# Moving the attention output's gatings between the weight splits, and turning the gate logits by full tiles

## The chip, the core and the metric

The kernel runs on one core of one Trainium2 chip. The metric is the device time of one execution in microseconds, shown as the median of the runs. A core has a matrix engine (PE), a vector engine (DVE), an activation engine (ACT), a general engine (POOL) and a queue engine (SP). Each takes its own instructions in order; semaphores tie them together. SP, ACT and POOL also issue DMA transfers, all of which run on the same 16 DMA engines.

## The reference, cut to what matters

The program is a trunk of two layers over 256 tokens of width 1024. Each layer normalises its input, projects it with one wide weight, runs two token mixers beside each other (a gated delta rule in both directions over chunks, here called branch a, and differential softmax attention, branch b), gates each, merges both and projects back.

```
proj = h @ w_in[l]
(q_a, k_a, v_a, ab_a, z_a, q_b, k_b, v_b, z_b, gate_a, gate_b) = jnp.split(proj, SPLIT_IDX, axis=-1)
y_a = gated_delta_branch(q_a, k_a, v_a, ab_a, z_a, ...)
y_b = diff_attention_branch(q_b, k_b, v_b, z_b, ...)     # rmsnorm(o) * (1 - lambda_init) * silu(z_b)
merged = (jax.nn.sigmoid(gate_a) * (y_a @ w_pa[l]) + jax.nn.sigmoid(gate_b) * (y_b @ w_pb[l]))
x = x + merged @ w_out[l]
```

Two pieces are touched by the change: `ab_a`, 32 columns that hold the logits of beta and of the decay g for 8 heads and two directions, and the last line of branch b, the gating of the attention output by silu(z_b) ahead of `w_pb`.

## The kernel before, in words

All matrix work is kept near float32: each weight of 256 rows by 512 columns (a "part", four to a projection, numbered kp 0 to 3) is loaded by SP as `raw`, rounded by ACT to `hi` (L308), and DVE takes the rest `lo = raw - hi` (L310). The activations `hT` are split the same way, and the PE adds hi·hi, hi·lo and lo·hi (L324 to L326). So every part costs one load, one ACT cast, one DVE subtraction and 12 matmuls of 128 by 512 (two 128-row blocks, two token tiles m, three products). `raw` has three buffers, `hi` and `lo` two each, so a part's load starts when the `lo` three parts earlier is done.

The order of instructions on each engine is set by the framework's list scheduler, which places instructions by its own estimate of time. The kernel steers it with `behind(x)`, which lets an instruction be placed only after instruction x on the same engine, and with `mark[name, kp]`, which keeps the pair (cast, subtraction) of a part.

The stage around the change is the projection of the two merge gates, `gb` and then `ga`. Between their matmuls the PE does the rest of branch a: `y64p`, `zt`, `y128p` and `zt` join the blocks of a triangular inverse U (`join`, L928 to L978), then for each group of four heads and each direction `y1p`, `sp`, `ks`, `y2p`, `qs` and `po` run the chunk recurrence (`chunks`, L992 to L1033). ACT copies each result out of PSUM: `A<-y1p` (L1000) is the left operand of `sp`, and `ktm<-sp` (L1006) that of `ks`. DVE turns 32 by 32 blocks of U into `T64` (L954), which `y128p` reads.

In the same stage DVE gates the attention output. It is held as `ob[i]`, with i the half of heads (0 or 1) and m the token tile, so four pieces (i, m). For each piece `gate_yb` does four products of 128 by 128 (L1197), a DVE turn into `zb` (L249, in `send`), one store of 256 KB to DRAM (`bny_yb<-zb`, L251) and four loads of 64 KB back (`zb<-bny_yb`, L257, in `fetch`). Store and loads are issued on POOL, and the loads wait for the store to land. `split_B` then makes `ybT`: ACT the upper part (L263), DVE the lower (L265), placed behind the casts and subtractions of `ga0` kp 2 and 3 and of `ga1` kp 2 and 3. `ybT` is first read by the projection `pb`, after all of `ga`. The POOL queue also carries the bounce of the query norms (`qdr<-qss` L1049, `qss<-qdr` L1052), which `key_sums` fills by squares `tb_q`.

The gate logits are made early in each layer: 16 matmuls give `abp`, 64 rows (two addends of 32 columns each) by 256 tokens; ACT copies it to `abT`; two matmuls of the 64-row `abT` with `id2`, two stacked 32 by 32 identities, turn it and add the two addends (L636); one DVE copy takes it to `ab` (L638).

Of the kernel before, what the change touches and what calls it, by code (L numbers as in the profile page):

```python
# [8 lines left out]
F32 = mybir.dt.float32  # L9
# [3 lines left out]
ALU = mybir.AluOpType  # L13
# [4 lines left out]
P = 128  # L18
DM = 1024
KT = DM // P  # L20
SEQ = 256
NM = SEQ // P
# [23 lines left out]
C_QB, C_KB, C_VB, C_ZB, C_GA, C_GB = 4128, 5152, 6176, 7200, 8224, 9248  # L46
# [3 lines left out]
def hybrid_encoder(  # L50
# [19 lines left out]
    V, S, G, T = nc.vector, nc.scalar, nc.gpsimd, nc.tensor  # L70

    def pool(name, bufs=1, space=None):
        kw = {} if space is None else {"space": space}
        return ctx.enter_context(tc.tile_pool(name=name, bufs=bufs, **kw))

    const = pool("const")
    wpool = pool("wpool")
    big = pool("big")
    work = pool("work", 2)
# [15 lines left out]
    def bank_c(name):  # L95
        return ps_c.tile([P, 512], F32, tag="c", name=name)
# [4 lines left out]
    def last(ap, n):  # L101
        return ap.unsqueeze(ap.ndim).to_broadcast(list(ap.shape) + [n])

    mark = {}


    ident = const.tile([P, P], F32, name="ident")
# [1 line left out]
    G.memset(ident, 1.0)  # L109
    G.affine_select(out=ident, in_=ident, compare_op=ALU.is_equal, fill=0.0,  # L110
                    base=0, pattern=[[1, P]], channel_multiplier=-1)
    id2 = const.tile([64, 32], F32, name="id2")
    V.tensor_tensor(id2, ident[0:64, 0:32], ident[0:64, 32:64], ALU.add)
    G.memset(tri, 1.0)
    for d, sg in ((0, 1), (1, -1)):
        G.affine_select(out=tri[:, d, :], in_=tri[:, d, :], compare_op=ALU.is_ge,
# [28 lines left out]
    def e4(name, tag):  # L145

        return [big.tile([P, NM, 512], F32, tag=tag, name=f"{name}_{i}", bufs=2) for i in range(2)]

    def heads4(ap):
        return ap.rearrange("p (h e) -> p h e", e=P)  # L150
# [103 lines left out]
    def fetch(tb, dd, after):  # L254
        for j in range(4):
            with behind(after):
                G.dma_start(out=tb[blk(j)], in_=dd[:, :, j].rearrange("i t x -> t i x"))  # L257
# [9 lines left out]
    def pair(nm):  # L267
        return [big.tile([P, 2, 4, SEQ], F32R, tag="p8", name=f"{nm}_{i}", bufs=4) for i in range(2)]

    def behind(ins):  # L270
        return nullcontext() if ins is None else tc.issue_after(ins)
# [43 lines left out]
    def proj_tm(act, w, c0, n, evac, nm, places=(None,) * 4, spare=(), later=None, turned=(), between=None,  # L315
                banks=None, held=None, first=(), raws={}):

        accs = (banks or banks2)(f"pp_{nm}")
        for kt, hi, lo in weights(w, c0, n, nm, places, later=later, spare=spare, turned=turned, held=held,
                                  first=first, raws=raws):  # L320
            for m in range(NM):
                ts_ = slice(m * P, (m + 1) * P)
                o = accs[m][:, :n]
                T.matmul(o, act[kt // 4][:, 0, kt % 4, ts_], hi, start=kt == 0, stop=False)  # L324
                T.matmul(o, act[kt // 4][:, 0, kt % 4, ts_], lo, start=False, stop=False)  # L325
                mark["proj"] = T.matmul(o, act[kt // 4][:, 1, kt % 4, ts_], hi, start=False,  # L326
                                        stop=kt == KT - 1).ins
                mark["done", nm, kt] = mark["proj"]
        if between:
            between()  # L330
        for m in range(NM):
            evac(m, accs[m][:, :n])
# [174 lines left out]
    for l in range(DEPTH):  # L507
# [109 lines left out]
        ab = small.tile([P, NM, 32], F32, tag="ab", name=f"ab{l}")  # L617
# [9 lines left out]
        abp = ps_p.tile([P, 512], F32, tag="p", name=f"abp{l}")  # L627
        for kt in range(KT):
            for part in range(2):
                T.matmul(abp[0:64, :SEQ], wabr[:, kt, :], hT[kt // 4][:, part, kt % 4, :],  # L630
                         start=kt == 0 and part == 0, stop=kt == KT - 1 and part == 1)
        abT = work.tile([64, SEQ], F32, tag="w2c", name=f"abT{l}", bufs=3)
        mark["ab"] = S.copy(abT, abp[0:64, :SEQ]).ins
        abq = bank_c(f"abq{l}")
        for m in range(NM):
            T.matmul(abq[:, m * 32 : (m + 1) * 32], abT[:, m * P : (m + 1) * P], id2,  # L636
                     start=True, stop=True)
        V.tensor_copy(ab.rearrange("p m c -> p (m c)"), abq[:, :64])  # L638

        a_ = small.tile([P, NM, 32], F32, tag="ga_", name=f"ga_{l}")  # L640
        V.tensor_scalar(a_[:, :, 0:16], ab[:, :, 0:16], -1.0, None, ALU.mult)
# [524 lines left out]
        for p in range(4):  # L1166
            z_part((zb, za)[p // 2], (C_ZB, C_ZA)[p // 2], ("zb", "za")[p // 2], p % 2)
            for h in (2 * p, 2 * p + 1):
                at = place((3, 7, 11, 15, 19, 23, 27, 31)[h])
# [21 lines left out]
        def gated(o_, z_, r_, nw_, yT, nm, tiles=range(NM), after={}, halves_=range(2), sent=None):  # L1191
            for i in halves_:
                for m in tiles:
                    zv, ov = heads4(z_[i][:, m, :]), o_(i, m)
                    for j in range(4):
                        with behind(after.get((i, m))):
                            V.scalar_tensor_tensor(ov[:, j, :], ov[:, j, :],  # L1197
                                                   r_[:, m, 4 * i + j : 4 * i + j + 1],
                                                   zv[:, j, :], ALU.mult, ALU.mult)
                    if sent is None:  # L1200
                        split_T(yT[i], ov, m, f"{nm}{i}", w=nw_)
                    else:
                        tb = z_[i][:, m, :].rearrange("p (j x) -> p j x", j=4)
                        sent[i, m] = tb, send(tb, ov, f"{nm}{i}{m}")

        def gate(c_base, nm, tag, between=(None, None), places=((None,) * 4,) * 2, first=(),
                 raws=({}, {})):
            gt = []
            for i in range(2):
                def evac_g(m, ps, i=i):  # L1210
                    if not gt:
                        gt.extend(e4(nm, tag))
                    S.activation(gt[i][:, m, :], ps, AF.Tanh, scale=0.5)
                proj_tm(hT, wl, c_base + 512 * i, 512, evac_g, f"{nm}{i}", places[i], between=between[i],
                        later={1: (0, None)} if i and places[i][1] is not None else None,
                        first=first, raws=raws[i])
            return gt
# [27 lines left out]
        V.scalar_tensor_tensor(rb, rb, 0.5 * (1.0 - lam0), r0, ALU.mult, ALU.mult)  # L1245

        ybT, yb_sent = pair(f"ybT{l}"), {}
        def gate_yb(i):
            at = [mark[f"ga{l}0", 1 + m][1] if i else mark[f"gb{l}1", 2 + m][1] for m in range(NM)]
            gated(lambda i, m: heads4(ob[i][:, m, :]), zb, rb, nw[:, 1:2], ybT, f"yb{l}",  # L1250
                  after={(i, m): at[m] for m in range(NM)}, halves_=(i,), sent=yb_sent)
            for m in range(NM):
                fetch(*yb_sent[i, m], None)

        gate_yb(0)
        gta = gate(C_GA, f"ga{l}", "eo", (lambda: gate_yb(1), None))
        for i, m in ((0, 0), (0, 1), (1, 0), (1, 1)):
            split_B(ybT[i], yb_sent[i, m][0], m, nw[:, 1:2], mark[f"ga{l}{i}", 2 + m])
        branch(ybT, w_pb[l], gtb, f"pb{l}")
# [73 lines left out]
        for s_, _ in enumerate(o_last):  # L1333
            if more:
                prenorm(s_, xt, wb, l + 1)
            else:

                m = min(s_, 1)
# [6 lines left out]
                else:  # L1345
                    cs = slice(256 * (s_ - 1), 256 * s_)
                    part = ss[:, 1:2] if s_ == 1 else small.tile([P, 1], F32, tag="xsl", name="xsl", bufs=1)
# [49 lines left out]
```

## Time and profile before

| | |
|---|---|
| median of 3 runs | 743.0 us (742.79 to 744.36) |
| the profiled execution | 742.73 us, span 740.8 us |
| granted clock of the matrix engine | 0.997 |
| PE busy | 732.1 us, 99% of the span, 5034 records |
| DVE, ACT, POOL busy | 588.5, 479.5, 140.9 us |
| gate stage, layer 0 (first `pp_ga` to last) | about 254 to 296 us |
| gate stage, layer 1 | about 616 to 658 us |

Matrix records overlap in the trace: a 128 by 512 product is shown with 0.39 us, but the next starts 0.23 us later. So what a step of the PE costs is read from the distance between starts. A float32 product is shown as two records ("x4" are two products), a turn by the PE as one.

### The profile page before, as it was taken

The numbers are of one execution on the slowest core, as the hardware profiler recorded it, in microseconds if no ns is written. First come the engines' busy times: TensorE is split into PE (matmuls) and PEld (weight loads), VectorE is DVE, ScalarE is ACT, GpSimd is POOL, SyncE is SP. The second block draws the span as 40 slices with busy tenths as digits, with TensorE's granted clock in tenths as the row PEclk, the third lists the DMA queues.
The fourth block names the chain that finished last, engine by engine and source line by source line (L and its number), as shares of the span: only waits on it lengthen the run. The fifth ranks groups of instructions, "written<-read, shape, count | busy, mean of one in ns | idle before, by whom it ended". The sixth has DMA issues, their size and how long they took to land.

```text
span 740.8 us, 13649 instructions
## 1 busy us (share of the span) xinstructions
PE 732.1 (99%) x5034; PEld 635.6 (86%) x5034; DVE 588.5 (79%) x1119; ACT 479.5 (65%) x1018; POOL 140.9 (19%) x223
## 2 busy tenths in 40 slices
PE   9999999999999999999999999999999999999996
PEld 6999889987888899888889899889788888998885
DVE  8696898999986885578667769999999769728782
ACT  6666875667876586645456578555787748665552
POOL 6004110112022433100000150202110514311000
PEclk9999999999999999999999999999999999999998
DMA  8755667776766473567674466767766736436641
GB/s 264 239 173 171 172 181 195 209 207 203 208 181 163 136 208 104 173 205 246 201 234 138 129 192 184 212 175 236 200 173 197 203 116 196 150 124 204 213 142 57
DMA packets 73732, 135.43 MB, mean 183 GB/s; under 512 B 12912, under 2 KB 13921, under 8 KB 73666
## 3 DMA queue, kind: packets, MB, share of 16 engines
q1 hardware_dynamic: 64750, 113.65, 51.6%
q0 software_dynamic: 7936, 19.35, 9.1%
q10 hardware_dynamic: 980, 1.58, 0.6%
q8 instruction: 39, 0.64, 0.4%
q14 instruction: 27, 0.22, 0.1%
HBM read 125.53 MB, written 9.01 MB: 182 GB/s over the span
## 4 chain that ended last, share of the span: by engine, by line
PE 96%; ACT 2%; issue 1%; DVE 1%; POOLq 0%; POOL 0%; DVEq 0%; ACTq 0%
PE pp_vb L369 4%; PE pp_qk L325 4%; PE pp_qk L326 3%; PE pp_qk L324 3%; PE sc L1067 2%; PE pp_o L369 2%; PE pp_za L325 2%; PE pf_k L385 2%; PE pf_v L385 2%; PE pf_v L389 2%; PE pp_ga L324 2%; PE pp_gb L324 2%; PE pp_zb L324 2%; PE pf_q L387 2%; PE pf_k L389 2%; PE pf_k L387 2%
## 5 line engine op out<-in xcount | busy, mean ns | idle before, releaser
L325 PE MATMUL pp_qk<-lo_qk,hT 128*128 128x512 f32 x128 | 50.5, 394 | 0.3
L326 PE MATMUL pp_qk<-hi_qk,hT 128*128 128x512 f32 x128 | 49.9, 390 | 0.0
L310 DVE TENSOR_TENSOR lo_qk<-raw_qk,hi_qk 128x1024 fp32r<-128x1024 f32 x32 | 39.1, 1221 | 12.0 <-ACT hi_qk L308 11.7
L324 PE MATMUL pp_qk<-hi_qk,hT 128*128 128x512 f32 x128 | 45.1, 393 | 0.0
L308 ACT CAST hi_qk<-raw_qk 128x1024 fp32r<-128x1024 f32 x28 | 29.4, 1049 | 23.4 <-PE pp_qk L326 12.7
L1077 ACT ACTIVATE es<-sc,mx 128x256 f32<-128x256 f32 x64 | 29.6, 473 | 19.5 <-DVE mx L1075 19.5
L385 PE MATMUL pf_q<-hT,hi_q 128*128 128x256 f32 x128 | 36.1, 285 | 0.0
L387 PE MATMUL pf_q<-hT,hi_q 128*128 128x256 f32 x128 | 35.9, 284 | 0.0
L385 PE MATMUL pf_k<-hT,hi_k 128*128 128x256 f32 x128 | 35.9, 286 | 0.0
L387 PE MATMUL pf_k<-hT,hi_k 128*128 128x256 f32 x128 | 35.9, 285 | 0.0
L385 PE MATMUL pf_v<-hT,hi_v 128*128 128x256 f32 x128 | 35.8, 285 | 0.0
L387 PE MATMUL pf_v<-hT,hi_v 128*128 128x256 f32 x128 | 35.8, 284 | 0.0
L389 PE MATMUL pf_q<-hT,lo_q 128*128 128x256 f32 x128 | 35.2, 288 | 0.0
L310 DVE TENSOR_TENSOR lo_pb<-raw_pb,hi_pb 128x1024 fp32r<-128x1024 f32 x16 | 19.6, 1225 | 18.9 <-ACT hi_pb L308 18.9
L389 PE MATMUL pf_v<-hT,lo_v 128*128 128x256 f32 x128 | 34.6, 288 | 0.0
L389 PE MATMUL pf_k<-hT,lo_k 128*128 128x256 f32 x128 | 34.3, 284 | 0.0
L308 ACT CAST hi_pa<-raw_pa 128x1024 fp32r<-128x1024 f32 x16 | 16.9, 1055 | 22.2 <-PE pp_pa L326 16.1
L679 DVE SCALAR_TENSOR_TENSOR cvq<-pf_q,cw,cvq 128x254 f32<-128x254 f32 (+1 forms) x64 | 30.0, 479 | 0.9 <-ACT cvq L675 0.4
L679 DVE SCALAR_TENSOR_TENSOR cvv<-pf_v,cw,cvv 128x254 f32<-128x254 f32 (+1 forms) x64 | 29.9, 479 | 0.1
L325 PEld LDWEIGHTS pp_qk<-lo_qk,hT 128*128 128x128 f32 x128 | 24.0, 188 | 6.6 <-DVE lo_qk L310 1.6
L679 DVE SCALAR_TENSOR_TENSOR cvk<-pf_k,cw,cvk 128x254 f32<-128x254 f32 (+1 forms) x64 | 28.5, 476 | 1.5 <-ACT cvk L675 0.9
L310 DVE TENSOR_TENSOR lo_pa<-raw_pa,hi_pa 128x1024 fp32r<-128x1024 f32 x16 | 19.6, 1224 | 11.2 <-ACT hi_pa L308 11.2
(416 smaller groups left out, 2535.1 us busy)
## 6 DMA issues: line engine op xcount, KB each, us to landing
raw_qk<-in_w_in_dram SPq DMA_DIRECT2D x32, 512.0 KB, 3.8
raw_k<-in_w_in_dram SPq DMA_DIRECT2D x16, 512.0 KB, 4.6
raw_q<-in_w_in_dram SPq DMA_DIRECT2D x16, 512.0 KB, 3.7
raw_v<-in_w_in_dram SPq DMA_DIRECT2D x16, 512.0 KB, 3.8
raw_zb<-in_w_in_dram SPq DMA_DIRECT2D x16, 512.0 KB, 4.0
raw_za<-in_w_in_dram SPq DMA_DIRECT2D x16, 512.0 KB, 3.8
raw_ga<-in_w_in_dram SPq DMA_DIRECT2D x16, 512.0 KB, 4.6
raw_pb<-in_w_pb_dram SPq DMA_DIRECT2D x16, 512.0 KB, 4.0
```

The source lines that it names most:

```text
L308: high = (V.tensor_copy if kp in turned else S.copy)(hi[:, :, :n], raw[:, :, :n]).ins
L310: mark[nm, kp] = high, V.tensor_tensor(lo[:, :, :n], raw[:, :, :n], hi[:, :, :n].bitcast(F32), ALU.subtract).ins
L324: T.matmul(o, act[kt // 4][:, 0, kt % 4, ts_], hi, start=kt == 0, stop=False)
L325: T.matmul(o, act[kt // 4][:, 0, kt % 4, ts_], lo, start=False, stop=False)
L326: mark["proj"] = T.matmul(o, act[kt // 4][:, 1, kt % 4, ts_], hi, start=False, stop=kt == KT - 1).ins
L369: mark["proj"] = T.matmul(o, act[kt // 4][:, pa, kt % 4, ts_], ws[kt][1 + pw], start=kt == 0 and n_ == 0, stop=kt == KT - 1 and n_ == 2).ins
L385: T.matmul(o, hi[:, cs], act[kt // 4][:, 0, kt % 4, :], start=first, stop=False, skip_group_check=True)
L387: T.matmul(o, hi[:, cs], act[kt // 4][:, 1, kt % 4, :], start=False, stop=False, skip_group_check=True)
L389: T.matmul(o, lo[:, cs], act[kt // 4][:, 0, kt % 4, :], start=False, stop=done, skip_group_check=True)
L679: V.scalar_tensor_tensor(ca[:, o0:o1], acc[:, b, o0 + sft : o1 + sft], cw[:, j, cb : cb + 1], ca[:, o0:o1], ALU.mult, ALU.add)
L1067: mm = T.matmul(sp[n][:, qt * SEQ : (qt + 1) * SEQ], qkT[h // 4][rows, 0, h % 4, qt * P : (qt + 1) * P], qkT[h // 4][rows, 1, h % 4, :], s ...
L1077: S.activation(es[:, n, qt, :], spv[:, qt, :], AF.Exp, bias=mx[:, n, qt : qt + 1], accum_out=s_all[:, h, n, qt : qt + 1])
```

## The change

Gatings: piece (0,0) stays behind the subtraction of `gb1` kp 2. Piece (0,1) moves from behind that of `gb1` kp 3 to behind that of `ga0` kp 0; (1,0) from kp 1 of `ga0` to kp 2, and (1,1) from kp 2 to kp 3. Each piece's store and loads are issued with it; before, both stores of i = 0 stood ahead of all eight loads. The places of `split_B` are as they were.

Gate logits: `abT` gets 128 rows, of which POOL sets the lower 64 to zero; two PE turns of full 128 by 128 tiles by the identity `ident` take the place of the two products with `id2`; DVE copies the first 32 columns and adds the second 32. `id2` and the instruction that made it go.

```diff
-    id2 = const.tile([64, 32], F32, name="id2")
-    V.tensor_tensor(id2, ident[0:64, 0:32], ident[0:64, 32:64], ALU.add)
...
-        abT = work.tile([64, SEQ], F32, tag="w2c", name=f"abT{l}", bufs=3)
-        mark["ab"] = S.copy(abT, abp[0:64, :SEQ]).ins
-        abq = bank_c(f"abq{l}")
+        abT = work.tile([P, SEQ], F32, tag="w2c", name=f"abT{l}", bufs=3)
+        G.memset(abT[64:P], 0.0)
+        mark["ab"] = S.copy(abT[0:64], abp[0:64, :SEQ]).ins
+        abq = bank_c(f"abq{l}")[:, :SEQ].rearrange("p (m c) -> p m c", m=NM)
         for m in range(NM):
-            T.matmul(abq[:, m * 32 : (m + 1) * 32], abT[:, m * P : (m + 1) * P], id2,
-                     start=True, stop=True)
-        V.tensor_copy(ab.rearrange("p m c -> p (m c)"), abq[:, :64])
+            T.transpose(abq[:, m, :], abT[:, m * P : (m + 1) * P], ident)
+        V.tensor_copy(ab, abq[:, :, 0:32])
+        V.tensor_tensor(ab, ab, abq[:, :, 32:64], ALU.add)
...
-        def gate_yb(i):
-            at = [mark[f"ga{l}0", 1 + m][1] if i else mark[f"gb{l}1", 2 + m][1] for m in range(NM)]
+        def gate_yb(i, m, at):
             gated(lambda i, m: heads4(ob[i][:, m, :]), zb, rb, nw[:, 1:2], ybT, f"yb{l}",
-                  after={(i, m): at[m] for m in range(NM)}, halves_=(i,), sent=yb_sent)
-            for m in range(NM):
-                fetch(*yb_sent[i, m], None)
-
-        gate_yb(0)
-        gta = gate(C_GA, f"ga{l}", "eo", (lambda: gate_yb(1), None))
+                  (m,), {(i, m): at}, (i,), yb_sent)
+            fetch(*yb_sent[i, m], None)
+
+        def gate_others():
+            for i, m, kp, part in ((0, 1, 0, 1), (1, 0, 2, 1), (1, 1, 3, 1)):
+                gate_yb(i, m, mark[f"ga{l}0", kp][part])
+
+        gate_yb(0, 0, mark[f"gb{l}1", 2][1])
+        gta = gate(C_GA, f"ga{l}", "eo", (gate_others, None))
```

What stands in the queues of layer 0, first on DVE from the end of `gb` on. Before:

```order
L1197 SCALAR_TENSOR_TENSOR ob_0_383<-ob_0_383,rb_2862,zb_0_385 128x128 x8
L249 STREAM_TRANSPOSE zb_0_385<-ob_0_383 128x4x4x32 x2
L954 STREAM_TRANSPOSE T_2651<-U__96 32x8x32 x2
L954 STREAM_TRANSPOSE T_2658<-U__96 32x8x32 x2
L310 TENSOR_TENSOR lo_ga_2896<-raw_ga_2897,hi_ga_2895 128x1024
L1004 TENSOR_TENSOR ktm_360<-ktm_360,kds_372 128x512 x2
L310 TENSOR_TENSOR lo_ga_2914<-raw_ga_2915,hi_ga_2913 128x1024
L1004 TENSOR_TENSOR ktm_360<-ktm_360,kds_372 128x512 x2
L1197 SCALAR_TENSOR_TENSOR ob_1_384<-ob_1_384,rb_2862,zb_1_386 128x128 x4
```

Now, over the same stretch (lines are one or two lower in the changed file):

```order
L1196 SCALAR_TENSOR_TENSOR ob_0_383<-ob_0_383,rb_2862,zb_0_385 128x128 x4
L247 STREAM_TRANSPOSE zb_0_385<-ob_0_383 128x4x4x32
L953 STREAM_TRANSPOSE T_2651<-U__94 32x8x32 x2
L953 STREAM_TRANSPOSE T_2658<-U__94 32x8x32 x2
L308 TENSOR_TENSOR lo_ga_2885<-raw_ga_2886,hi_ga_2884 128x1024
L1003 TENSOR_TENSOR ktm_360<-ktm_360,kds_372 128x512 x2
L1196 SCALAR_TENSOR_TENSOR ob_0_383<-ob_0_383,rb_2862,zb_0_385 128x128 x4
L308 TENSOR_TENSOR lo_ga_2903<-raw_ga_2904,hi_ga_2902 128x1024
L1003 TENSOR_TENSOR ktm_360<-ktm_360,kds_372 128x512 x2
L247 STREAM_TRANSPOSE zb_0_385<-ob_0_383 128x4x4x32
```

The four products and the turn of piece (0,1) have left the place ahead of the `T64` turns; the products stand behind `lo` of kp 0, the turn behind `lo` of kp 1 and four `ktm` products.

On ACT, behind the copies of `zt`, where `ybT_0` is the upper part of pieces (0,0) and (0,1) and `A<-y1p` are the copies that `sp` reads. Before:

```order
L263 ACTIVATE ybT_0_2869<-zb_0_385,nw_308 128x4x128
L308 CAST hi_ga_2995<-raw_ga_2997 128x1024
L1000 COPY A_370<-y1p_3477 128x512
L1046 ACTIVATE tb_q_3455<-tb_q_3455 128x512
L1000 COPY A_370<-y1p_3489 128x512
L1046 ACTIVATE tb_q_3459<-tb_q_3459 128x512
L1046 ACTIVATE tb_q_3463<-tb_q_3463 128x512
L1000 COPY A_370<-y1p_3495 128x512
L1000 COPY A_370<-y1p_3483 128x512
```

Now:

```order
L306 CAST hi_ga_2995<-raw_ga_2997 128x1024
L261 ACTIVATE ybT_0_2869<-zb_0_385,nw_306 128x4x128
L1045 ACTIVATE tb_q_3455<-tb_q_3455 128x512
L999 COPY A_370<-y1p_3477 128x512
L999 COPY A_370<-y1p_3489 128x512
L1045 ACTIVATE tb_q_3459<-tb_q_3459 128x512
L1045 ACTIVATE tb_q_3463<-tb_q_3463 128x512
L999 COPY A_370<-y1p_3495 128x512
L999 COPY A_370<-y1p_3483 128x512
```

The upper part of piece (0,1) still stands ahead of all four `A<-y1p` copies, now with a cast less between them.

On the PE, around `sp`, whose rows read `A`. Before, with `ga0` kp 3 as `hi_ga_2949`:

```order
L992 MATMUL sp_3502<-A_370,ktm_360 128x128 x4
L324 MATMUL pp_ga_2893<-hi_ga_2949,hT_1_127 128x512
L325 MATMUL pp_ga_2893<-lo_ga_2950,hT_1_127 128x512
L326 MATMUL pp_ga_2893<-hi_ga_2949,hT_1_127 128x512
L324 MATMUL pp_ga_2894<-hi_ga_2949,hT_1_127 128x512
L325 MATMUL pp_ga_2894<-lo_ga_2950,hT_1_127 128x512
L326 MATMUL pp_ga_2894<-hi_ga_2949,hT_1_127 128x512
L992 MATMUL sp_3516<-A_370,ktm_360 128x128 x4
```

Now, with `ga1` kp 0 as `hi_ga_2995`:

```order
L324 MATMUL pp_ga_2883<-hi_ga_2938,hT_1_125 128x512
L322 MATMUL pp_ga_2993<-hi_ga_2995,hT_0_124 128x512
L991 MATMUL sp_3502<-A_370,ktm_360 128x128 x2
L991 MATMUL sp_3516<-A_370,ktm_360 128x128 x2
L991 MATMUL sp_3502<-A_370,ktm_360 128x128
L991 MATMUL sp_3516<-A_370,ktm_360 128x128
```

`sp` now begins behind all 48 products of `ga0` and one of `ga1`. The second group of `zt` (64 by 64) has moved up by seven products. On POOL each store is followed by its own four loads; ahead of the last four loads, those of piece (1,1), now stand the zeroing of the next layer's `abT`, the store `qdr<-qss` and, in layer 0, a small load `lp`. Layer 1 shows the same moves.

## The prediction

> **What bounds the kernel now.** I read the page's busy times first, then the shares of the chain of waits.
>
> ```profile
> span 740.8 us, 13649 instructions
> PE 732.1 (99%) x5034; PEld 635.6 (86%) x5034; DVE 588.5 (79%) x1119; ACT 479.5 (65%) x1018; POOL 140.9 (19%) x223
> PE 96%; ACT 2%; issue 1%; DVE 1%; POOLq 0%; POOL 0%; DVEq 0%; ACTq 0%
> ```
>
> The PE is busy for all but 8.7 of 740.8 us and the chain lies on it for 96%. So an edit counts in two ways only: it changes the PE's own time, or it makes the PE wait. Work on DVE (79%), ACT and POOL is free until the PE waits for its result. But a busy PE may be a slow one: where its instructions wait briefly for data, the records close up, and the wait shows as a group that takes longer than its like. I therefore measure from start to start, and compare groups of one shape.
>
> **Gate logits: what goes and what comes.** The PE timeline (start, duration, engine, line, operation) shows the place in layer 0:
>
> ```profile
> 27.17 0.28 PE L389 MATMUL pf_k<-hT,lo_k 128*128 128x256 f32 x1
> 27.38 0.63 PE L636 MATMUL abq<-id,abT 64*128 64x32 f32 x4
> 27.94 0.39 PE L385 MATMUL pf_k<-hT,hi_k 128*128 128x256 f32 x1
> 28.16 0.28 PE L387 MATMUL pf_k<-hT,hi_k 128*128 128x256 f32 x1
> 28.28 0.28 PE L389 MATMUL pf_k<-hT,lo_k 128*128 128x256 f32 x1
> ```
>
> From 27.17 to 28.28, 1.11 us, the PE passes `L389`, both `abq` products (four records, two passes each), `L385` and `L387`. One `pf_k` product is 28.28 − 28.16 = 0.12 from start to start; three are 0.36, so the two `abq` products cost 0.75. They are the only ones here on a tile of 64 by 128 rather than 128 by 128. Two full turns of the new kind stand elsewhere among the same products:
>
> ```profile
> 45.50 0.28 PE L385 MATMUL pf_k<-hT,hi_k 128*128 128x256 f32 x1
> 45.62 0.38 PE L706 MATMUL ctk<-ident,kq 128*128 128x128 f32 x2
> ...
> 46.08 0.28 PE L385 MATMUL pf_k<-hT,hi_k 128*128 128x256 f32 x1
> L706 PE MATMUL ctk<-ident,kq x32: 270/272/273, 45.6 to 432.1; 128*128 128x128 f32 x32
> ```
>
> From 45.50 to 46.08, 0.58 us, it passes `L385`, two turns and one each of `L387` and `L389` (the rows left out). Less 0.36, two turns cost 0.22, or 0.11 each. The gain is 0.75 − 0.22 = 0.53 per layer, **−1.06** for two. The last row gives the record of one turn as 0.272 us (minimum, median and maximum are 270, 272 and 273 ns); records overlap, so 0.11 is what the PE loses. If the whole record counted, the gain would be 1.50 − 4 × 0.272 = 0.41: the small end.
>
> The Trainium skill, "TensorE: Matmul & The Clock Gate", section "Part 4: PE-mode transpose", measures a full turn at about 390 ns alone and about 275 ns inside one kernel. The trace agrees with 275 as the length of a record (272), not as the step (0.11); by 390 ns the four turns would cost 1.56 us and gain nothing, and by 275 as a step the time would be that of rival 2.
>
> The zeroing on POOL (19% busy) and the second DVE instruction lie beside PE work: the `abT` copy on ACT is not moved. Without that cover they would cost their own length, some tenths of a microsecond.
>
> **Gatings: what they free.** Before, eight products and two turns stand on DVE ahead of the `T64` turns, which `y128p` reads. DVE, ACT and the chain:
>
> ```profile
> 246.79 2.19 DVE L1197 SCALAR_TENSOR_TENSOR ob<-ob,rb,zb 128x128 f32<-128x128 f32 x8
> 248.90 1.99 DVE L249 STREAM_TRANSPOSE zb<-ob 128x512 f32<-128x512 f32 x2
> 250.92 1.84 DVE L954 STREAM_TRANSPOSE T<-U__96 32x256 f32<-32x256 f32 x4
> 252.79 1.23 DVE L310 TENSOR_TENSOR lo_ga<-raw_ga,hi_ga 128x1024 fp32r<-128x1024 f32 x1
> 253.93 1.29 DVE L1004 TENSOR_TENSOR ktm<-ktm,kds 128x512 f32<-128x512 f32 x2
> 247.97 3.17 ACT L951 ACTIVATE U__96<-zt 32x256 f32<-32x256 f32 x8 [4.14 <-PE zt L943]
> 251.16 1.05 ACT L308 CAST hi_ga<-raw_ga 128x1024 fp32r<-128x1024 f32 x1
> 252.29 0.61 PE y128p L961 x17
> 252.90 1.11 PE y128p L961 x44
> 259.02 1.10 PE zt L961 x64
> ```
>
> The turns end at 250.92 + 1.84 = 252.76, after `y128p` has begun. Its first 17 records take 0.036 us each, up to 252.90, the others 0.025: an excess of 17 × 0.011 = 0.18 us, all of it waiting for `T64`. In all it takes 1.72, against 1.10 for 64 products of `zt`, so the bounds are 0 and 0.62. I take 0.18, from the rows that change pace just where the turns end: **−0.36** for two layers. Now four products (1.1) and one turn (1.0) stand ahead; the four `U` copies that the turns read end halfway through the eight, at 249.6. `T64` is then ready near 251, over 1 us early.
>
> A second pair of groups runs slow, in layer 0 only. Chain, layer 0 and then layer 1, and the DVE row beside it:
>
> ```profile
> 285.64 1.07 PE y2p L992 x8
> 286.71 1.26 PE qs L992 x10
> 648.05 0.89 PE y2p L992 x8
> 648.95 1.12 PE qs L992 x10
> 284.20 0.27 DVE L1053 TENSOR_REDUCE ssq<-qss 128x16 f32<-128x64 f32 x1 [2.53 <-DMA qss<-qdr]
> ```
>
> DVE sits 2.53 us before the `ssq` sum for a load from `qdr`, with the `vtm` updates that these groups read queued behind it. The groups take 0.18 and 0.14 longer than in layer 1. In the changed order `ssq` stands behind those updates: **−0.32**, with bounds 0 (the slowness has another cause) and 0.32.
>
> **Gatings: what they may cost.** Piece (0,1) is now made later and needed as before. On DVE its store waits for the following, from `hi_ga` (ACT, 251.16 + 1.05, ready at 252.2): `lo` 1.2, two `ktm` 1.2, four products 1.1, `lo` 1.2, two `ktm` 1.2, its turn 1.0, which is 259.1 and, with the gaps, about 259.3. Before, it was ready by 250.92, so 8 us are given up. The second `lo` ends at 257.0 by this count, and the PE is still in the products of the first kp and `zt` until 258 or so.
>
> Queued behind the wait for its return is ACT: the upper `ybT` of (0,1) stands ahead of the four `A<-y1p` copies, for which `sp` waits on the PE. ACT and chain, before:
>
> ```profile
> 264.35 1.27 ACT L263 ACTIVATE ybT<-zb,nw 128x512 fp32r<-128x512 f32 x1
> 265.50 1.05 ACT L308 CAST hi_ga<-raw_ga 128x1024 fp32r<-128x1024 f32 x1
> 266.44 0.59 ACT L1000 COPY A<-y1p 128x512 f32<-128x512 f32 x1
> ...
> 267.44 0.59 ACT L1000 COPY A<-y1p 128x512 f32<-128x512 f32 x1
> ...
> 268.96 1.07 ACT L1000 COPY A<-y1p 128x512 f32<-128x512 f32 x2
> 270.96 2.68 PE sp L992 x24
> ```
>
> From the start of `ybT`, less the cast's 266.44 − 265.50 = 0.94 (now ahead of it), two copies are done after 268.03 − 264.35 − 0.94 = 2.74 and all four after 270.03 − 264.35 − 0.94 = 4.74. On the PE one `sp` product is 2.68/24 = 0.112; now all 32 (3.57) stand behind one `pp_ga` product more (0.23), so they begin at 273.64 + 0.23 − 3.57 = 270.3, and need the other two copies after 16 of them, at 272.1. Both give 267.4 to 267.6 as the latest start of `ybT`. So store to last landing may take 267.5 − 259.3 = **8.2 us** for nothing. What it takes, from POOL, the landing times of these buffers and the windows (PE, PEld, DVE, ACT, POOL busy, clock, DMA share, GB/s):
>
> ```profile
> 250.28 0.65 POOL L251 DMA_DIRECT2D bny_yb<-zb  x1 [3.73 <-DVE zb L249]
> 252.98 4.36 POOL L257 DMA_DIRECT2D zb<-bny_yb  x8 [1.25 <-DMA bny_yb<-zb]
> 260.08 0.56 POOL L251 DMA_DIRECT2D bny_yb<-zb  x1 [2.73 <-DMA wb_n<-in_norm_w_dram]
> 265.41 2.17 POOL L257 DMA_DIRECT2D zb<-bny_yb  x4 [4.77 <-DMA bny_yb<-zb]
> DMA to landing us min/median/max: 2.1/4.0/7.2
> 247.00:256.00 9.00, 9.00 (x199) 7.44 (x187) 8.84 (x18) 7.73 (x15) 4.22 (x8) 1.00 0.31 90
> 256.00:264.00 8.00, 8.00 (x97) 6.53 (x96) 7.88 (x15) 5.28 (x7) 1.91 (x4) 1.00 1.00 301
> ```
>
> Store to first load takes 2.7 us (250.28 to 252.98) with quiet DMA engines and 5.3 (260.08 to 265.41) with full ones; three more issues take 1.6 of the 2.17; a landing 2.1 to 7.2. The low end is 2.7 + 1.6 + 2.1 = 6.4. The high end, 5.3 + 1.6 + 5 = 12, takes full DMA engines for both ways, with a landing between median and maximum; it stalls 3.8 us per layer. I take about 7.5 and so nothing: the store of 260.08 had eight loads of piece (0,0) and (0,1) going out just ahead, which are now four and earlier. This is the weakest step, since 259.3 lies where the share is 1.00.
>
> Piece (1,0) has the same path as before, two steps of `ga0` later. The last loads, those of (1,1), now stand on POOL behind a zeroing, a store and a small load: three instructions of about 0.55 (as `L257`, 2.17 for four), 1.6 us. Bounds: 0 if the upper `ybT` of (1,1) still finds them landed, 1.6 us per layer if it is waited for at once. I take 0: `pp_pb`, which reads the piece, comes behind all of `ga1`, so only ACT's work behind it could be held.
>
> **Sum.** −1.06 − 0.36 − 0.32 = −1.74 against the profiled execution's own 742.73: 741.0. The median, 743.0, lies 0.27 above that execution, so **741.3**.
>
> **Rivals.**
>
> 1. *The round trip of (0,1) comes too late* (slower from a point on). ACT waits at `ybT`, the `A<-y1p` copies follow late, the PE stands before `sp`, in both layers. For it: the DMA share of 1.00 from 256 to 264 and the 5.3 us. Against: half the loads ahead. Each us beyond 267.5 costs 1 us per layer. Past 0.87 per layer (landing after 268.4) the gain of 1.74 is gone, past 1.6 (after 269.1) the kernel is measurably slower. Typical 0.7: 741.3 + 1.4 = 742.7; at 1.4 it is 744.1; the far end, 3.8, gives 748.9.
> 2. *A turn costs its record, 0.272*. For it: four turns close together have no such row. Against: the step of 0.11. Gain 0.41 in place of 1.06: 742.0.
> 3. *The gate logits' gain is taken back.* About 4% of the chain lies on other engines or on issue; if the chain next passes there at an unchanged time, the 1.06 disappears: 742.3. Against: ACT and DVE work mostly hangs on PE results that move up too.
>
> **Numbers.** A measurement here tells no change from a difference of about 0.2%, 1.5 us: 741.5 and 744.5. Forecast without a new stall 0.58 (own range 740.4 to 742.0: `y128p` at its bound of 0.62 takes off 0.88 more, both stalls at 0 give back 0.68): 0.43 faster, 0.15 within. Rival 1 0.32: 0.16 within, 0.16 slower. Rivals 2 and 3 0.05 each, within. Together 0.43, 0.41, 0.16. The range runs from 740.4 into rival 1, to 744.3, leaving out its upper half.
>
> **What would show it.** Right: the span from `pf_k` to `pf_k` around `abq` falls from 1.11 to near 0.6; `y128p` in 1.5 us or less in one even group; `y2p` 0.89 and `qs` 1.12 in layer 0; no PE wait before `sp`. Wrong: an ACT wait at `ybT` for loads of `bny_yb`, landing after 267.5, and `sp` groups over 0.9 per eight, or `T64` still ending after `y128p` begins.

## The result: slower, by the return of one piece

The changed kernel takes 745.83 us (median of 6 runs, 745.36 to 746.38), the kernel before 742.7 (6 runs, 742.07 to 744.36). The ratio is 1.004, with an interval of 1.0028 to 1.0052: a loss of 0.4%, small but clear of the noise. The forecast was 741.3, with a range up to 744.3: the time lies outside, on the side of rival 1, and further out than its typical case.

The page of the changed kernel, its span, its busy times and its chain of waits:

```profile
span 744.1 us, 13644 instructions
PE 734.0 (99%) x5030; PEld 637.1 (86%) x5030; DVE 589.4 (79%) x1120; ACT 479.4 (64%) x1018; POOL 139.8 (19%) x225
PE 91%; issue 3%; ACT 2%; DMA 1%; DVE 1%; POOL 1%; POOLq 0%; DVEq 0%; ACTq 0%
```

The PE still reads 99%, but the chain has left it: 91% where it was 96%, and DMA and POOL are in it now. Where it leaves the PE, in layer 1, the chain reads (start, duration, what):

```profile
622.66 4.72 DMA bny_yb<-zb
627.38 1.84 issue
629.22 1.34 POOL zb L255 x3
630.56 0.28 issue
630.84 2.12 DMA zb<-bny_yb
...
633.06 0.30 ACT ybT L261
...
634.16 0.61 ACT tb_q L1045
634.78 0.48 ACT A L999
...
635.30 0.71 PE sp L991 x4
```

This is rival 1 from its first step to its last: the store of piece (0,1), the issue of its loads, the last landing, `ybT` on ACT, the copies into `A`, and `sp` on the PE. The same in layer 0 is seen on POOL and ACT, and at the end the PE wait that the view of waits names:

```profile
260.54 0.56 POOL L249 DMA_DIRECT2D bny_yb<-zb  x1 [5.20 <-DVE zb L247]
263.76 2.17 POOL L255 DMA_DIRECT2D zb<-bny_yb  x4 [2.66 <-DMA bny_yb<-zb]
```

```profile
269.03 1.24 ACT L261 ACTIVATE ybT<-zb,nw 128x512 fp32r<-128x512 f32 x1 [3.06 <-DMA zb<-bny_yb]
...
633.06 1.20 ACT L261 ACTIVATE ybT<-zb,nw 128x512 fp32r<-128x512 f32 x1 [4.96 <-DMA zb<-bny_yb]
```

```profile
PE sp L991 <- ACT A L999: 1.8, 1, 1.8
```

ACT sat idle 3.06 and 4.96 us for the loads. The wait view counts 1.8 us of PE time, all in layer 1; more is hidden in the pace of `sp` itself, which has the form that the prediction warned of: 32 records in 4.22 us in layer 0 (chain, below) where 32 × 0.112 = 3.57 would do. (What the prediction calls 32 products of `sp` and 64 of `zt` are records, two to a product; its sums go by records and stand.)

To see where the time went I paired each PE instruction of the changed kernel with the same one before (same operands, in order of time) and took the median difference of starts in each 10 us. It changes at a few places only:

```
place (time before)        step     sum
first products, 0 to 15    +1.57   +1.57
abq, layer 0               -0.53   +1.03
(drift from 30 to 249)     +0.11   +1.14
y128p, layer 0             -0.29   +0.85
zt (64 by 64), layer 0     +0.29   +1.14
sp, layer 0                +0.65   +1.79
y2p and qs, layer 0        -0.35   +1.44
abq, layer 1               -0.52   +0.88
y128p, layer 1             -0.20   +0.69
zt and sp, layer 1         +2.69   +3.38
```

The sums between are measured too; the last is the difference of the spans, 3.3, as near as such medians go. In layer 1 `zt` takes 0.28 of the last step, from the start of its group to the product behind it (1.38 us against 1.10), and `sp` about 2.4. Three of the places were in the sum (`abq`, `y128p`, `y2p` with `qs`), one was a rival (`sp`), and two had no price in the prediction: `zt`, and the first 15 us.

The groups behind the terms, in the changed kernel. PE timeline at `abq`, layer 0:

```profile
28.73 0.28 PE L387 MATMUL pf_k<-hT,lo_k 128*128 128x256 f32 x1
28.85 0.38 PE L635 MATMUL abq<-ident,abT 128*128 128x128 f32 x2
28.99 0.36 PE L383 MATMUL pf_k<-hT,hi_k 128*128 128x256 f32 x1
29.19 0.28 PE L385 MATMUL pf_k<-hT,hi_k 128*128 128x256 f32 x1
29.31 0.28 PE L387 MATMUL pf_k<-hT,lo_k 128*128 128x256 f32 x1
```

From 28.73 to 29.31 is 0.58 us where it was 1.11. The chain at the small products of layer 0, and at the groups that ran slow before:

```profile
253.46 1.41 PE y128p L960 x61
...
258.29 1.37 PE zt L960 x60
...
271.42 4.22 PE sp L991 x32
...
287.65 0.89 PE y2p L991 x8
288.55 1.12 PE qs L991 x10
```

`y128p` is one even group of 1.41 instead of 0.61 and 1.11; `zt` has gone from 1.10 to 1.37; `y2p` and `qs` are at their pace of layer 1.

### The profile page after: what moved, and what is told of

It reads as the page before. It is cut to its first block, busy times and chain, and to the rows that moved or that the text cites. A ratio compares the mean times of both kernels' runs of the same rounds, so it can differ in the third digit from the quotient of the medians.

```text
span 744.1 us, 13644 instructions
## 1 busy us (share of the span) xinstructions
PE 734.0 (99%) x5030; PEld 637.1 (86%) x5030; DVE 589.4 (79%) x1120; ACT 479.4 (64%) x1018; POOL 139.8 (19%) x225
## 4 chain that ended last, share of the span: by engine, by line
PE 91%; issue 3%; ACT 2%; DMA 1%; DVE 1%; POOL 1%; POOLq 0%; DVEq 0%; ACTq 0%
PE pp_vb L367 4%; PE pp_qk L323 4%; PE pp_qk L324 3%; PE pp_qk L322 3%; PE sc L1066 2%; PE pp_o L367 2%; PE pf_v L383 2%; PE pp_za L323 2%; PE pf_k L383 2%; PE pf_v L387 2%; PE pp_zb L322 2%; PE pf_k L387 2%; PE pf_q L385 2%; PE pf_k L385 2%; PE pf_v L385 2%
```

## The experiments

Theory after this result: two sound gains (turns, and the small products), given back by the round trip of piece (0,1) in both layers, through ACT's order. The first rival: the order of the DVE, or the turns, does the damage, and the wait on ACT only goes along with it. All times are medians; the kernel before was run beside each.

**One part at a time.** `e1_turn` is the kernel before with the gate logits' part of the diff alone, `e2_gate` with the gatings' part alone.

> The kernel before with the gate logits' part alone (turns of full tiles, the instruction that made id2 gone). Theory: the turn takes 0.53 us off each layer, -1.06 together, and nothing else moves: 742.7 - 1.06 = 741.6. The PE rows of the changed kernel lose 1.57 us before 9 us, where its first products step at 0.213 us as against 0.111 before: if that belongs to the removed DVE instruction, this run shows it too and comes to 743.2; if it is chance of the single execution, the profile here may go either way and the time stays near 741.6.

> The kernel before with the gatings' part alone. Theory: y128p gains 0.32 per layer, zt (64 by 64) loses 0.28 per layer by its new inner order (eight records of one bank, then eight of the other), y2p and qs gain 0.35 in layer 0, and the late return of piece (0,1) stalls sp by 0.65 in layer 0 and 2.4 in layer 1: 742.7 - 0.64 + 0.56 - 0.35 + 3.05 = 745.3. If the stall before sp came from elsewhere (the turns), no stall here and 742.3.

`e1_turn` took 741.4 us (ratio 0.9987, 0.9978 to 0.9996), `e2_gate` 746.3 (1.0046, 1.0033 to 1.0058). The turn is a gain by itself, the gatings a loss by themselves. In `e2_gate` ACT waited the same way, 4.85 and 4.54 us at `ybT`, and the PE before `sp`:

```profile
PE sp L992 <- ACT A L1000: 3.0, 2, 1.6
```

**The wait taken off ACT's path.** `e3_late` leaves the gatings where the change put them, and issues `ybT` of (0,1) behind the second kp of `ga1`, so the `A` copies no longer queue behind it:

```diff
-            split_B(ybT[i], yb_sent[i, m][0], m, nw[:, 1:2], mark[f"ga{l}{i}", 2 + m])
+            split_B(ybT[i], yb_sent[i, m][0], m, nw[:, 1:2],
+                    mark[f"ga{l}1", 1] if (i, m) == (0, 1) else mark[f"ga{l}{i}", 2 + m])
```

> The changed kernel with both parts of ybT of piece (0,1) issued behind the second kp of ga1 in place of the fourth of ga0, so that the four A copies do not stand behind the wait for its return on ACT. Theory: the stall before sp (3.05 us in both layers) goes, all else stays: 742.7 - 1.06 - 0.64 + 0.56 - 0.35 = 741.2, or 742.8 if the slow start belongs to the change. Rival: the wait only moves, to ACT's casts of ga1 and so to the PE, and 744 or more remains.

It took 741.54 (0.9986, 0.9977 to 0.9995). No PE wait for `A` is left, and `sp` takes its 3.57 us in both layers, though POOL issues the loads as late as in the changed kernel (4.6 and 6.5 us after the store):

```profile
263.77 2.18 POOL L255 DMA_DIRECT2D zb<-bny_yb  x4 [4.06 <-DMA bny_yb<-zb]
269.80 3.57 PE sp L991 x32
627.13 2.18 POOL L255 DMA_DIRECT2D zb<-bny_yb  x4 [5.94 <-issue]
631.31 3.57 PE sp L991 x32
```

So the loss is this one queueing on ACT. How large it is depends on the execution. The medians differ by 745.83 − 741.54 = 4.3 us, but the profiled execution of the changed kernel, as long as its median, also began late (last section): paired as above with the profiled execution of `e3_late`, 1.4 of their 4.7 us lie before 20 us and the rest, some 3.3, at `sp` and just behind it in the two layers. `e2_gate` began early and paid more at `sp`: 3.0 idle, and 4.33 instead of 3.57 in each layer, 4.5 in all. How the other executions of the changed kernel divide is not known, since no trace of them was kept.

**Piece (0,1) put back.** `e4_back` is the changed kernel with (0,1) behind `gb1` kp 3 again; (1,0) and (1,1) stay moved:

```diff
-            for i, m, kp, part in ((0, 1, 0, 1), (1, 0, 2, 1), (1, 1, 3, 1)):
+            for i, m, kp, part in ((1, 0, 2, 1), (1, 1, 3, 1)):
...
+        gate_yb(0, 1, mark[f"gb{l}1", 3][1])
```

> The changed kernel with piece (0,1) back behind the fourth kp of gb1 (pieces (1,0) and (1,1) stay moved). Theory: no stall before sp, y128p slow again (1.72 us from start to end per layer), zt in the old inner order (1.10): 742.7 - 1.06 - 0.35 = 741.3, or 742.9 with the slow start. Rival: pieces (1,0) and (1,1), later by a kp, cost by themselves; then the time stays above 743.

741.62 (0.9985, 0.9976 to 0.9994). The other two pieces cost nothing that can be measured.

**The consumer earlier.** `e7_later` was meant to send (0,1) later, behind kp 1 of `ga0`:

```diff
-            for i, m, kp, part in ((0, 1, 0, 1), (1, 0, 2, 1), (1, 1, 3, 1)):
+            for i, m, kp, part in ((0, 1, 1, 1), (1, 0, 2, 1), (1, 1, 3, 1)):
```

> The changed kernel with piece (0,1) one kp later still, behind the second lower part of ga0 (zt then stands in its old inner order, -0.56). Theory, round trip of (0,1) sets sp: its store goes out 2 to 2.4 us later in each layer and every us is paid: 745.83 - 0.56 + 4.4 = 749.7. Rival, sp waits for something else: 745.3.

749.32 (1.0083, 1.0053 to 1.0114; four executions: 744.36, 748.77, 749.87, 751.15). The median came near 749.7, but not for the reason written. The turn had stood behind the `lo` of kp 1 already, and against the work around it the store went out only 0.1 us later. What moved is the other end: with `zt` back in its old place, the first `sp` products stand five `pp_ga` products earlier on the PE, 5 × 0.23 = 1.15 us, so there is that much less cover in front of the wait. The one trace is that of the 744.36. In layer 0 the return took 6.9 us and the PE did not wait; in layer 1 it took 10.1 and the PE waited:

```profile
632.88 1.16 PE L991 MATMUL sp<-A,ktm 128*128 128x128 f32 x8 [2.44 <-ACT A L999]
```

The other three executions were granted a clock of 0.993 to 0.994, the traced one 0.999. Span times granted clock is 741.8 us for the traced one and 742.2 to 743.9 for the others, so most of the 4 to 7 us between them goes with the clock. Whether longer waits lowered the clock is not shown. That the median met the forecast was luck.

**Why the return is long.** Issue of the store, then how long the store took to land, how long POOL took from there to issue the first load, how long the last load took to land, and the whole up to the start of `ybT` (the first and the last load are issued 1.6 us apart; landings by the semaphores in the traces):

```
kernel, layer     store   lands   to load   last lands   whole
after, 0         260.54    2.9      0.28        3.5       8.5
after, 1         622.66    4.7      1.84        2.1      10.4
e2_gate, 0       258.94    4.6      0.28        3.7      10.3
e2_gate, 1       623.35    2.9      1.83        3.6      10.0
e7_later, 0      259.46    2.8      0.28        2.1       6.9
e7_later, 1      621.08    2.7      1.84        3.8      10.1
e10_noraw, 0     259.24    2.9      0.28        2.1       7.0
e10_noraw, 1     620.66    2.8      1.84        2.1       8.5
```

Two parts of the return take one of two lengths, and a third goes by the layer. A store lands in 2.7 to 2.9 us or in 4.3 to 4.7 (`e3_late`, where nothing waits for it, has 4.3 and 4.7), the last load in 2.1 to 2.2 or in 3.5 to 3.8, and in layer 1 POOL issues the first load 1.84 us after the store's landing where 0.28 do in layer 0. The last is the same to 0.01 us in all four kernels, and in `e3_late` too, whatever the DMA engines and DVE are doing, so it is no matter of traffic.

`e10_noraw` takes the raw loads of `ga1` kp 0 and 1 out of the DMA engines. Their casts read the raw tile of the last kp of `ga0` instead, so these two quarters of the weights are left out of the computation; the order on the PE is that of the changed kernel to the row.

```diff
+                again = nm[:2] == "ga" and nm[-1] == "1" and kp < 2
+                if again:
+                    raw = mark["raw"]
...
-                    mark["load", nm, kp] = (nc
+                    if not again: mark["load", nm, kp] = (nc
```

> The changed kernel without the raw loads of kp 0 and 1 of ga1 (both kp are cast from the raw tile of the last kp of ga0, so their weights are left out of the computation; every instruction on PE stays in place). Theory, the return of piece (0,1) is long because its packets wait behind raw loads: the round trip falls to 6.5 us or so (2.7 to the loads, 1.6 of issues, 2.2 landing), the stall before sp goes, 741.5. Rival, the round trip is that long by itself: 745.5.

742.82 (1.0002, 0.9989 to 1.0014; ten runs from 741.16 to 745.71): 3.0 us below the changed kernel in the median, but short of 741.5. In the profiled execution no wait of the PE for `A` is left, and `sp` takes 3.57 us in layer 0 and 4.15 in layer 1. Paired with the changed kernel, it saves 0.65 us at `sp` of layer 0 and 1.9 at that of layer 1, besides 1.3 at the start.

Only layer 0 speaks for the theory. There the changed kernel issues the left-out raw load at 265.59, 0.2 us after the last of the four loads; without it that load lands in 2.1 us instead of 3.5. The other rows fit: the loads took 3.5 to 3.8 wherever the last of them was issued between 0.2 us before and 1.6 us after this raw load, and 2.1 to 2.2 elsewhere (`e3_late` has 3.6 and 2.2). In layer 1 the changed kernel issues the left-out load at 627.60, when its store has already landed, at 627.38. In both kernels SP issues the raw loads ahead of that at the same distances from the store (5.9 and 2.5 us before it, 0.8 after it), and yet the store landed in 2.8 us here and in 4.7 there. So the 1.9 us of layer 1 is not the work of the load left out there; `e2_gate` and `e7_later` show 2.9 and 2.7 with every load kept. How much of the 3.0 us between the medians is the edit's is not known. The 1.84 us of POOL stayed:

```profile
620.66 0.56 POOL L249 DMA_DIRECT2D bny_yb<-zb  x1 [4.97 <-DVE zb L247]
625.34 2.17 POOL L255 DMA_DIRECT2D zb<-bny_yb  x4 [4.11 <-issue]
```

The packet records show how a store comes to land late. Data packets begun in each half us, layer 1, by queue, with `e10_noraw` shifted by 2 us so that the stores stand beside each other:

```
changed kernel                        e10_noraw
from      POOL's queue   SP's queue   from     POOL's queue   SP's queue
622.5          0             52       620.5         0             65
623.0          0             83       621.0         0             84
623.5         14             77       621.5        14             57
624.0         29             30       622.0        36             24
624.5         10             20       622.5        14             13
625.0          7             30       623.0         0             46
625.5          1             54       623.5         0             77
626.0          1             79       624.0         0             72
626.5          2             50       624.5         0             28
```

The store gets its 64 packets through when SP's queue slackens. In `e10_noraw` all have begun before the next raw load comes; in the changed kernel 11 have not, and its last begin after 626.5 while that raw load passes. The Trainium skill, "DMA: Bandwidth & Descriptors", section "Queues, rings and completion order", lets an engine alternate between its queues packet by packet; how such an even share leads to a tail of a few packets that waits 2 us, and why some stores make the gap and others do not, is not shown by these runs.

`e9_actq` sends the store and the loads of (0,1) on ACT's hardware queue:

```diff
-                        sent[i, m] = tb, send(tb, ov, f"{nm}{i}{m}")
+                        sent[i, m] = tb, send(tb, ov, f"{nm}{i}{m}", nc.scalar if (i, m) == (0, 1) else None)
```

> The changed kernel with the store and the four loads of piece (0,1) issued by ACT on its own hardware queue, in place of POOL. To be read from the trace: store issue to the landing of the last load. On POOL's queue it was 8.5 to 10.4 us in the changed kernel. Theory, POOL's packets are held back while the raw loads of SP's queue move: the hardware queue does better, 5 to 7 us in all (issues not counted). Rival, the DMA engines are simply full: 8 us or more again. The time itself is not the point: ACT is blocked while it waits for the turn and for the store, and I expect 745 to 752.

One execution, 743.66, below the expected range. From the store at 258.91 the first load went out at 262.15, and `ybT` followed at 267.14; in layer 1 at 622.25, 624.78 and 629.34:

```profile
622.25 0.35 ACTq L249 DMA_DIRECT2D bny_yb<-zb  x1
624.78 0.80 ACTq L255 DMA_DIRECT2D zb<-bny_yb  x2
...
625.73 0.89 ACTq L255 DMA_DIRECT2D zb<-bny_yb  x2
...
629.34 1.26 ACT L261 ACTIVATE ybT<-zb,nw 128x512 fp32r<-128x512 f32 x1 [0.21 <-DMA zb<-bny_yb]
```

That is 8.2 and 7.1 in all, where POOL's queue took 8.5 and 10.4. But the store and the last load by themselves took 3.2 + 3.4 and 2.5 + 3.1 us to land, against 2.9 + 3.5 and 4.7 + 2.1: the same in layer 0, shorter in layer 1, and within what POOL's queue shows elsewhere. Most of the rest is that ACT issues the first load 0.02 us after the landing, and the 1.84 us of POOL does not arise. The traffic was not the same either: the second raw load that SP issues behind the store goes out 9.0 and 8.2 us after it, not 5.1 and 4.9. So the run does not tell whether packets fare better on the hardware queue. It cost elsewhere: ACT stood still for the store's landing, and `y1p` waited for `U` copies.

**The pace of the small products.** `zt` had slowed though nothing waited. The order of the rows told why: before, its products go by turns, two of one bank and two of the other; in the changed kernel it begins with eight of one and eight of the other, as `y128p` always did, and goes on by twos. `e11_alt1` is `e3_late` with the products of `y128p` alone held in written order, which goes by turns; nothing else moves on any engine but one small copy on DVE at the start.

```diff
+                last = mark["pin"]
                 for c, j4, g, d in every4:
-                    with behind(mark["pin"]):
-                        T.matmul(ps[g][halves[1 - row(d) if g == 0 else row(d)], c, j4, :],
...
+                    with behind(last):
+                        made = T.matmul(ps[g][halves[1 - row(d) if g == 0 else row(d)], c, j4, :],
...
+                    if ps is y128p:
+                        last = made
```

> As e3_late, with the products of y128p alone by turns of two and two; all other orders are those of e3_late. Theory, inner order sets the pace: y128p from 1.40 to 1.10 in each layer, 741.54 - 0.6 = 740.9. Rival, no effect: 741.5.

740.75 (0.9974, 0.9963 to 0.9985), the lowest median of the study. `y128p` fell from 1.41 to 1.09 us in both layers:

```profile
253.41 1.09 PE y128p L961 x64
...
614.50 1.09 PE y128p L961 x64
```

Two others tried it on both groups. `e6_alt_late` holds `y128p` and `zt` of `e3_late`, `e5_alt_turn` those of `e1_turn`:

> As e3_late, with the products of y128p and zt by turns. Theory: y128p 1.40 to 1.10 and zt 1.38 to 1.10 in each layer: 741.54 - 1.16 = 740.4. Rival, order without effect: 741.5.

> Turn of the gate logits alone (as e1_turn), with the 32 products of y128p and of zt (64 by 64) each held in written order, two of one bank and two of the other by turns, where y128p before had eight and eight. Theory: the inner order sets the pace (zt takes 1.38 us from its first product to what follows it with eight and eight, 1.10 by turns), so y128p falls from 1.72 to about 1.4, its T64 stall staying: 741.4 - 0.6 = 740.8. Rival: the order does nothing and zt was slow for another reason, no change.

`e6_alt_late` took 741.12 (0.9986, 0.9977 to 0.9995), `e5_alt_turn` 742.38 (1.0003, 0.9994 to 1.0011). The order did what it should; the chain of `e6_alt_late` shows `y128p` at the pace of `zt`:

```profile
251.81 1.09 PE y128p L961 x64
...
258.82 1.08 PE zt L961 x60
```

But its `zt` was torn into 4 and 60 records with `pp_ga` products between, and the 4 stood 0.27 us on the PE by themselves (256.22 to 256.49), which ate most of the gain. `e5_alt_turn`, expected at 740.8, came out 1.0 us above `e1_turn`. There `y128p` gained nothing: its turns `T64` still came late, now seen openly as a wait. `zt` was torn in the same way and lost 0.24 in each layer; where the rest of the 1.0 went was not settled. The wait:

```profile
251.86 0.47 PE L961 MATMUL y128p<-T,A 64*64 64x64 f32 x6
252.51 1.11 PE L961 MATMUL y128p<-T,A 64*64 64x64 f32 x58 [0.17 <-DVE T L953]
```

**What the turn saves.** `e8_plain` is `e3_late` with plain products by `id2` again, on `abT` padded to 128 rows:

```diff
-            T.transpose(abq[:, m, :], abT[:, m * P : (m + 1) * P], ident)
+            T.matmul(abq[:, m, 0:32], abT[:, m * P : (m + 1) * P], id2, start=True, stop=True)
```

> As e3_late, with the gate logits by plain products again (id2), but on abT padded to 128 rows: tile 128 by 128, no turn, no second add on DVE. If the 0.75 us of the two products came from their 64-row tile among full tiles, the stretch around abq takes about 0.58 here too and the time is that of e3_late, 741.5; if it came from the plain fp32 product against the turn, the stretch takes 1.11 again and the time is 742.6.

741.55 (0.9988, 0.9979 to 0.9998). The stretch lies between the two expected values:

```profile
27.57 0.28 PE L390 MATMUL pf_k<-hT,lo_k 128*128 128x256 f32 x1
27.69 0.53 PE L638 MATMUL abq<-id,abT 128*128 128x32 f32 x4
28.05 0.36 PE L386 MATMUL pf_k<-hT,hi_k 128*128 128x256 f32 x1
28.25 0.28 PE L388 MATMUL pf_k<-hT,hi_k 128*128 128x256 f32 x1
28.37 0.28 PE L390 MATMUL pf_k<-hT,lo_k 128*128 128x256 f32 x1
```

28.37 − 27.57 = 0.80, less three products of 0.12, is 0.44 for the two. So of the 0.75 us before, 0.31 came from the 64-row tile among full ones, and 0.22 from the second pass of a plain product, which a turn does not need (two records, not four). The time, 741.55, cannot tell these 0.22 per layer; the rows do.

## Why the prediction was wrong, step by step

- **Gate logits, −0.53 per layer: right.** Measured −0.53 and −0.52; the step of 0.11 from the `ctk` rows was the price, not the record of 0.272 (rival 2), and nothing took the gain back (rival 3). `e1_turn` is faster by 0.13%, some 1.0 us.
- **`y128p`, −0.18 per layer: mechanism right, size small.** Its `T64` stall was worth 1.72 − 1.41 = 0.31. The whole group, not only its first 17 records, had been slowed. The upper bound of 0.62 mixed two things: the stall, and the inner order that `e11_alt1` took away (0.3 more).
- **`zt`: a missing term, +0.28 per layer.** It was known that the group moves up by seven products, and the prediction gave the move no price. Its inner order had changed with it, which stands in the order of the rows (a group of eight and one of eight where there were threes and twos) and was not read. Gatings' gain on the PE, `y128p` and `zt` together, is then nearly nothing.
- **`y2p` and `qs`, −0.32: the size was right, the reason unsound.** The changed kernel shows −0.35. But `e1_turn`, where `ssq` stands ahead of the `vtm` updates as before, shows −0.35 too, as the load from `qdr` landed earlier in that execution:

```profile
283.07 0.27 DVE L1052 TENSOR_REDUCE ssq<-qss 128x16 f32<-128x64 f32 x1 [1.86 <-DMA qss<-qdr]
```

  DVE reached it at the same point and waited 1.86 us instead of 2.53. As far as two executions show, the term was the landing time of one transfer in one of them, not a property of the kernel before. That the sum came out here was luck.
- **The round trip of (0,1): the step that failed.** "I take about 7.5 and so nothing." It took 8.5 and 10.4 (and 6.9 to 10.3 in the experiments that kept all loads, mean 9.4 of six). The path was right, and so was the budget: with 0.65 and about 2.4 us of stall the harmless part was 8.5 − 0.65 = 7.9 and 10.4 − 2.4 = 8.0, where 8.2 was worked out. What was mis-sized is the time of the return, on the argument that fewer loads would go out just ahead of the store; the row at 260.08 and the DMA share of 1.00 spoke against it and were set aside. In layer 0 the landing of the loads was long, 3.5 us where the low end had 2.1. In layer 1 it was the landing of the store, 4.7, and POOL's 1.84 us between that landing and the first load, which had 0.3 in the sum, as the rows of layer 0 show it. Rival 1's typical price of 0.7 per layer became 0.65 and 2.4 in the profiled execution.
- **The sum without that step** would have been 741.3, and the kernels that are the change without its stall took 741.54 (`e3_late`) and 741.62 (`e4_back`). So the rest of the sum held in total, with `zt` against it and, in `e3_late`, `y128p` for it.

## What to carry to other kernels

A transfer that is moved later must be priced by the worst of its like in the same stretch, because an engine that takes its instructions in order, standing between it and the bottleneck, turned each us past the budget into a us of the kernel here; the cheap cure is to move the waiting instruction behind its queue's other work, not the transfer back. When a scheduler decides the order, compare the order inside every group that moved, not its place alone. A term that comes from one DMA wait in one profiled execution is worth its chance, not its full length.

## What was not expected of the hardware

**The inner order of quarter-array products.** 64 by 64 products that alternate between the two banks take 1.09 to 1.10 us per group of 64 records; where the first sixteen go eight and eight, the group takes 1.37 to 1.41. The indices in `quarters` (the line in the diff of `e11_alt1`, where `g` is the bank) tell which quarter of the array each uses: the products of one bank lie on one diagonal pair of quarters, those of the other bank on the other pair, so by turns all four are in use. `e11_alt1` shows the effect of the order; that the quarters are its reason is argued from the code, and since bank and quarters change together, no run parts the two. In the records before, `zt` starts four in each 0.058 us; in the changed kernel parts of it, at its start and end above all, start two in the same 0.058. The Trainium skill, "TensorE: Matmul & The Clock Gate", section "Part 3: Packing small matmuls — row/col tiling", says that products on different tile positions run at the same time; the trace agrees, with four products begun within 0.058 us, and here only where the order brings the positions close together.

**The first 10 us differ from execution to execution.** In the changed kernel's profiled execution the first products keep a step of 0.213 us until 10.1; before, it falls to 0.111 after 6.2 (six products in 0.94 us against 1.65):

```profile
6.18 0.60 PE L435 MATMUL pos<-ones,pos_r 1*128 1x1 f32 x4
6.71 0.94 PE L452 MATMUL pos<-ones 128*128 128x128 f32 x6
7.48 1.04 PE L227 MATMUL pt_h<-ident,h_n 128*128 128x128 f32 x8
```

```profile
6.24 1.01 PE L433 MATMUL pos<-ones,pos_r 1*128 1x1 f32 x4
7.18 1.65 PE L450 MATMUL pos<-ones 128*128 128x128 f32 x6
```

This made 1.57 of the 3.3 us between the two profiles, and is not the change's: `e1_turn`, which has the same opening, shows the early step, and `e11_alt1` the late one, in an execution of 741.92 where its median is 740.75. The clock column of the page shows nothing of it, but the clock records in the traces do: they begin, at full clock, at 5.91 us in the kernel before, 6.28 in `e1_turn`, 10.53 in the changed kernel and 10.88 in `e11_alt1`, just where the step changes. In the other nine traces they begin between 4.5 and 6.9. The Trainium skill, same page, section "Part 1: The HAM clock gate (the "warmup" mystery)", has the gate watch free-running windows, so that the release shifts from run to run, by ±500 ns. The traces agree that it shifts, but between kernels of one opening, `e1_turn` and the changed kernel, it is 4.25 us apart, much more than the page says. Two profiles must be aligned after it before they are compared.

**Open.** What the chain calls "issue" in layer 1, the 1.84 us between the store's landing (627.38) and POOL's first load (629.22), was not found. It is the same in five kernels and stands in layer 1 alone; in the kernel before, the load followed the landing at 626.62 by 0.5. Open too is why a store among the same raw loads lands in 2.8 us in one execution and in 4.7 in another.
